# Another order of the block sums in the Winograd product of a hybrid decoder trunk, and shorter filler between its HGRN2 cores' steps

## The chip, the core and the metric

The kernel runs on one core of one Trainium2 chip. Its engines run side by side, each with its own queue: TensorE (PE in the profile, its weight loads PEld), VectorE (DVE), ScalarE (ACT), GpSimd (POOL) and SyncE (SP), which issues the transfers from HBM. The time is the device time of one execution in microseconds; the median of three executions is compared.

## What is computed

A decoder trunk of two layers over 512 tokens with 1024 features. Layer 0 mixes tokens with a Mamba-2 state-space mixer, layer 1 with HGRN2; each layer then has a squared-ReLU MLP and a gate with an embedding of its own. The change touches the border of the two layers and the HGRN2 mixer. Of the reference, cut to this:

```python
for i in range(DEPTH):
    mix = ssd_mixer(x, ...) if i % 2 == 0 else hgrn2_mixer(x, ...)
    h = layer_norm(DEEPNORM_ALPHA * x + mix, ...)
    h = layer_norm(DEEPNORM_ALPHA * h + sq_relu_mlp(h, w1, w2), ...)
    x = h + jax.nn.sigmoid(h @ ple_w_gate[i]) * (p[i] @ ple_w_proj[i])

def hgrn2_mixer(u, w_in, lb, norm_w, w_out):
    q, fz, v, g = jnp.split(u @ w_in, 4, axis=-1)
    k = (1.0 - lb) * jax.nn.sigmoid(-fz)          # and log_f, the decay
    # per head: causal scores of q and k under the decay, times v; state from chunk to chunk
    ...
    o = rms_norm(o, norm_w) * jax.nn.silu(g)
    return o @ w_out
```

## The kernel before

Every float32 product is made of three matmuls on operands that are split into a high and a low part (`mm3`, L118 to L120: high by high, high by low, low by high). ACT writes a high part, DVE subtracts it from the value for the low part. For weights `unit` loads a piece of 128 x 1024 through SP (L105) and `split` makes the parts (L112 on ACT, L114 on DVE).

The instructions of an engine stand in an order that a planner makes beforehand: among those that are ready, the one that comes first in the program goes first, and `tc.high_priority(offset=n)` lets an instruction count as n places earlier. Within `tc.manual_schedule` for PE (around the call of `values4`, L814, and around the cores, L1069) TensorE's own order is that of the program; the other engines' orders are still planned.

**The gate of layer 0** (`mlp_and_gate`, L464 to L502) works through two halves of the features, h, and four token chunks, c. After each chunk's output the chunk before it is transposed (`turn`, L442): four transposes by TensorE (L447), the high part of the transposed tokens (L450, ACT), a float32 copy into `rows` (L451, ACT) and the low part (L452, DVE). `rows[0]` holds tokens 0 to 255, `rows[1]` tokens 256 to 511, each with both halves of the features. The last `turn`, of h = 1 and c = 3, is left over in `late`.

**`values4`** (L505) computes the values and output gates of the first four HGRN2 heads, X W with X of 512 tokens x 1024 features, by seven products of blocks (Winograd's form of Strassen's method) in place of eight. The blocks of X are a11 and a12 (tokens 0 to 255, first and second half of the features) and a21 and a22 (tokens 256 to 511), views of `rows`, 128 x 1024 each in memory. The products in TensorE's order, 24 matmuls each: a11 (then the left-over `turn`), a12, s3, s2, a22, s1, s4, where

- s1 = a21 + a22
- s2 = s1 - a11
- s3 = a11 - a21
- s4 = a12 - s2

`put` (L512) splits a sum into a buffer of the pool `b8` (L514 on ACT, L515 on DVE). The sums of the weights t1 to t4 are made by `weight_sums` (L314) and split in `sums(t)`. `first` (L532, ACT) and `more` (L535, DVE) take results out of PSUM; at the end a Silu is applied to the gates' half (L560, ACT).

**The HGRN2 cores.** `hcore` (L930) handles two heads; it runs four times, for heads 0, 2, 4 and 6. It has 15 steps, after each of which it yields: seven levels m = 0 to 6 (L949 and L963 are the matmuls of levels 0 to 4, L970 of levels 5 and 6; DVE scales with L983 and L984; ACT copies scores with L1006 after level 4 and with L1012 at levels 5 and 6), two steps of transposed keys (L1019, copied by L1021), two of states `sv` (L1030, L1032, L1034), two of outputs `po` (L1043, L1045, squares and square root L1050 and L1051 on ACT, L1055 on DVE) and two of transposed outputs `ot` (L1063, taken out by L1064 on ACT and L1065 on DVE, through the one bank `pt`).

Between the steps TensorE gets filler from `background`: the projections of the next heads, q0 to q7 (`qf`, 16 pieces each), the values of the last four heads, v2 and v3 (`vg`, 32 pieces each), and the first half of the output projection, o (`out0`, 32 pieces). A piece is one `mm3` of three matmuls of 512 columns and counts as 0.65. `fill(n)` adds n to a credit and takes pieces while it is positive. The n of a step is its entry of `FILL`, in the fourth core times LAST = 0.78; before the first core q0 and q1 are made and 6.0 (`AHEAD`) filled. What a job leaves for ACT when its last matmul is done is its tail: four activations for a `qf` (L880, L881, L883, L884), copies and Silus for a `vg` (L861, L863). What the background has left after the fourth core runs then; the second half of the output projection (`out_project`, L82) isn't under the manual order and is planned into TensorE's free places.

Of the kernel before, what the change touches and what calls it, by code (L numbers as in the profile page):

```python
# [27 lines left out]
RAWS = 3  # L28
FIRST = 1000
SOON = 40  # L30

PERIODS = ("TTTTTTTT",) + 3 * ("TTQTQTQTQTQTQTQ",) + ("QQQQQQQ",)
SUMS = (60, 300, 300, 300)

JOBS = "q2 q3 q4 q5 v2 q6 q7 v3 o".split()
FILL = (3.15, 1.1, 1.35, 1.95, 2.4)
VALUE_SUMS = 60
AHEAD = 6.0
LAST = 0.78
# [4 lines left out]
def trunk(ctx: ExitStack, tc, a):  # L44
    nc = tc.nc
# [21 lines left out]
    def mk(p, shape, tag, dt=F32, **kw):  # L67
        return p.tile(list(shape), dt, tag=tag, name=nm(tag), **kw)

    def f32(t):  # L70
        return t.bitcast(F32)
# [19 lines left out]
    def bank(p, tag):  # L91
        return mk(p, [P, T], tag)
# [8 lines left out]
    def unit(src, lead=LEAD):  # L101
        n = src.shape[1]
        with tc.high_priority(offset=lead):
            raw = mk(raws, [P, 1024], "raw")
            nc.sync.dma_start(raw[:, :n], src)  # L105
        return split(raw[:, :n], lead)

    def split(f, lead=LEAD):
        n = f.shape[1]
        with tc.high_priority(offset=lead):  # L110
            hi = mk(whip, [P, 1024], "whi", F32R)
            nc.scalar.copy(hi[:, :n], f)  # L112
            lo = mk(wlop, [P, 1024], "wlo", F32R)
            nc.vector.tensor_sub(lo[:, :n], f, f32(hi[:, :n]))  # L114
        return hi, lo

    def mm3(out, sh, sl, mh, ml, start, stop, **kw):
        nc.tensor.matmul(out, sh, mh, start=start, stop=False, **kw)  # L118
        nc.tensor.matmul(out, sh, ml, start=False, stop=False, **kw)  # L119
        nc.tensor.matmul(out, sl, mh, start=False, stop=stop, **kw)  # L120
# [77 lines left out]
    def layer_norm(c, gb, sums=None):  # L198

        src = acc[:, c, :]  # L200
        mv = mk(sm, [P, 2], "lnmv")
        sd = mk(sm, [P, 1], "lnsd")
        if sums is None:
            st = mk(sm, [P, 2, 6], "lnst")
            for h in range(2):
                nc.vector.bn_stats(st[:, h, :], src[:, h * 512 : (h + 1) * 512])
            nc.vector.bn_aggr(mv, st.rearrange("p a b -> p (a b)"))
            nc.scalar.activation(sd, mv[:, 1:2], AF.Sqrt, bias=eps)
        else:

            nc.vector.tensor_scalar(mv[:, 0:1], sums[:, c, 0:1], sums[:, c, 1:2], -1.0 / D, ALU.add, ALU.mult)
            sq = mk(sm, [P, 2], "lnsq")
            for h in range(2):
                nc.scalar.activation(
                    tmp("sg", [P, T]), src[:, h * 512 : (h + 1) * 512], AF.Square, bias=mv[:, 0:1], accum_out=sq[:, h : h + 1]
                )
            nc.vector.tensor_add(mv[:, 1:2], sq[:, 0:1], sq[:, 1:2])
            nc.scalar.activation(sd, mv[:, 1:2], AF.Sqrt, scale=1.0 / D, bias=eps)
        rs = mk(sm, [P, 1], "lnrs")
        nc.vector.reciprocal(rs, sd)  # L220
        shift = ALU.subtract if sums is None else ALU.add
        nc.vector.scalar_tensor_tensor(src, src, mv[:, 0:1], gb[0], shift, ALU.mult)
        nc.vector.scalar_tensor_tensor(src, src, rs, gb[1], ALU.mult, ALU.add)

    def transpose_split(src, dst, c):

        sl = slice(c * P, (c + 1) * P)
        for q in range(2):
# [5 lines left out]
            h = dst.hi[q][:, :, sl]  # L234
            with tc.high_priority(offset=SOON):
                nc.scalar.copy(h, v)  # L236
# [3 lines left out]
    def out_part(units, n, xs, c, h, first, scale, last=False, sums=None):  # L240
# [8 lines left out]
        d = acc[:, c, h * 512 : (h + 1) * 512]  # L249
        with tc.high_priority(offset=SOON if last else 0):  # L250
            if scale is not None:
# [25 lines left out]
    def norm(i):  # L277
# [5 lines left out]
        def chunk(c):  # L283
            with tc.high_priority(offset=SOON if c < 2 or i % 2 == 0 else 0):
                layer_norm(c, gb, sums)
# [28 lines left out]
    def weight_sums(w, lead, eng=nc.vector):  # L314

        t = [[None, None] for _ in range(4)]

        def load(i, u, src):
            t[i][u] = tmp("r", [P, 1024])
            nc.sync.dma_start(t[i][u], src)  # L320

        with tc.high_priority(offset=lead):
            for u in range(2):
                load(0, u, w[0][1][u])
                load(2, u, w[1][1][u])
                eng.tensor_sub(t[2][u], t[2][u], t[0][u])
                load(1, u, w[0][0][u])
                eng.tensor_sub(t[0][u], t[0][u], t[1][u])
                eng.tensor_add(t[1][u], t[2][u], t[1][u])
            for u in range(2):  # L330
                load(3, u, w[1][0][u])
                eng.tensor_sub(t[3][u], t[3][u], t[1][u])
        return t

    def block_product(w, blk, lead, first, after=None, turns=None, sums=None):
# [7 lines left out]
        def product(x, f, name, start, i, j, turns=None):  # L343
# [4 lines left out]
            for c in range(2):  # L348
# [9 lines left out]
                d = acc[:, 2 - 2 * i + c, j * 512 : (j + 1) * 512]  # L358
                with tc.high_priority(offset=SOON if after else 0):
                    if after and f in (w[1][0], t1, t4, w[1][1]):  # L360
# [144 lines left out]
    def values4(xs, rows, late):  # L505

        w = [[[a["whvg"][4 * j + 2 * i + u] for u in range(2)] for j in range(2)] for i in range(2)]
        t1, t2, t3, t4 = weight_sums(w, VALUE_SUMS, nc.vector)
        a11, a12, a21, a22 = (rows[i][:, j] for i in range(2) for j in range(2))
        res = [[mk(w4, [P, 2, T], "ab"[i]) for i in range(2)] for _ in range(2)]  # L510

        def put(f):  # L512
            t = mk(b8, [P, 2, 4, 256], "b8", F32R)
            nc.scalar.copy(t[:, 0], f)  # L514
            nc.vector.tensor_sub(t[:, 1], f, f32(t[:, 0]))  # L515
            return lambda k, c: tuple(t[:, i, k, c * P : (c + 1) * P] for i in range(2))

        def part(i, j):
            sl = lambda c: slice((2 * i + c) * P, (2 * i + c + 1) * P)
            return lambda k, c: (xs.h(4 * j + k, sl(c)), xs.l(4 * j + k, sl(c)))  # L520

        def product(x, us, banks, start, drain):
            for c in range(2):
                for k in range(4):
                    hi, lo = us[k // 2]
                    ks = slice(k % 2 * T, (k % 2 + 1) * T)
                    mm3(banks[c], *x(k, c), hi[:, ks], lo[:, ks], start and k == 0, k == 3, skip_group_check=True)
                with tc.high_priority(offset=SOON):
                    drain(c, banks[c])

        def first(i, j):
            return lambda c, ps: nc.scalar.copy(res[j][i][:, c], ps)  # L532

        def more(i, j):
            return lambda c, ps: nc.vector.tensor_add(res[j][i][:, c], ps, res[j][i][:, c])  # L535

        pair = lambda: [bank(psj, "pj") for _ in range(2)]
        sums = lambda t: [split(v) for v in t]
        x, z, y = [bank(psy, "py%d" % c) for c in range(2)], pair(), pair()
        product(part(0, 0), [unit(v) for v in w[0][0]], x, True, first(0, 0))  # L540
        for f in late:
            f()
        nc.vector.tensor_add(a22, a21, a22)
        nc.vector.tensor_sub(a21, a11, a21)
        s3 = put(a21)
        product(part(0, 1), [unit(v) for v in w[1][0]], z, True, more(0, 0))
        nc.vector.tensor_sub(a11, a22, a11)
        s2 = put(a11)
        product(s3, sums(t3), y, True, first(1, 1))
        product(s2, sums(t2), x, False, first(1, 0))  # L550
        s1 = put(a22)
        product(part(1, 1), sums(t4), y, False, more(1, 0))
        nc.vector.tensor_sub(a12, a12, a11)
        s4 = put(a12)
        product(s1, sums(t1), x, False, more(1, 1))
        product(s4, [unit(v) for v in w[1][1]], x, False, first(0, 1))
        for j in range(2):
            for i in range(2):
                g = res[j][i][:, :, 256:]
                nc.scalar.activation(g, g, AF.Silu)  # L560
            made["vg", j] = res[j]
# [368 lines left out]
    def hcore(h0, s, i0):  # L930
# [22 lines left out]
        for m in range(NLEV):  # L953
# [35 lines left out]
            for r in R:  # L989
# [17 lines left out]
                else:  # L1007
                    pc = pc[:, base(half) : base(half) + 2 * half].rearrange("p (c l) -> p c l", c=2)
                    for b in range(0, P, 2 * half):
                        for odd in range(2):  # L1010
                            row = b + half * odd
                            nc.scalar.copy(sc[b : b + half, odd::2, b + half : b + 2 * half], pc[row : row + half])  # L1012
            yield FILL[0]

        kt = []
        for r in R:
# [4 lines left out]
            nc.scalar.copy(kt[r], pt[:, : 3 * P].rearrange("p (c k) -> p c k", c=3))  # L1021
            yield FILL[1]
        res = need("vg", h0 // 2)
# [3 lines left out]
        for r in R:  # L1027
# [5 lines left out]
            for c in range(1, 3):  # L1033
                nc.vector.scalar_tensor_tensor(  # L1034
                    sv[r][:, c], sv[r][:, c - 1], tot[r][:, c : c + 1], pss[:, c * P : (c + 1) * P], ALU.mult, ALU.add
                )
            yield FILL[2]
        os = []
        for r in R:
# [18 lines left out]
            os.append(o)  # L1058
            yield FILL[3]
        for r in R:  # L1060
# [4 lines left out]
            nc.vector.scalar_tensor_tensor(s.l(i0 + r), pt, hnw[:, 0:1], f32(s.h(i0 + r)), ALU.mult, ALU.subtract)  # L1065
            yield FILL[4]

# [136 lines left out]
```

## Time and profile before

| | |
|---|---|
| median of 3 executions | 1437.37 us (1437.36 to 1441.27) |
| the profiled execution | 1437.35 us, its span 1435.5 us |
| mean granted clock of TensorE | 0.997 |
| transfers | 176.69 MB on the queue for data, 35.6% of 16 DMA engines' time |
| the gate of layer 0 (its last part) | about 715 to 765 us |
| `values4` | about 765 to 811 us |
| the four cores with their filler | about 840 to 1026 us |

Times within the execution are counted from the span's start. An instruction on a line of a helper, such as L118, belongs to whoever called it, so the tiles' names tell the place: `pj` and `py` are PSUM banks, `whi` and `wlo` the parts of weights, `b` the pool of split tokens, `blk` the rows. [...]

### The profile page before, as it was taken

To read this page: it belongs to the slowest core of one execution; us is meant where nothing else is said; L and a number is where in the kernel's file an instruction comes from. 1 tells how busy PE (TensorE), PEld (TensorE's weight loads), DVE (VectorE), ACT (ScalarE), POOL (GpSimd) and SP (SyncE) were. 2 spreads that over 40 slices of the span, in tenths; PEclk is the share of its full clock that TensorE was granted. 3 is DMA by queue.
4 is the path that set the end of the run, shared out by engine and by line. 5 is a ranking of instruction groups with operands and counts; after the bars stand their busy time and mean duration, and the time that the engine had idled before them with its cause. 6 is when DMAs were issued, how large, how long until landed. Compare 5 with 4: busy or idle time off the path is not lost.

```text
span 1435.5 us, 20976 instructions
## 1 busy us (share of the span) xinstructions
PE 1420.1 (99%) x8381; PEld 1175.9 (82%) x8381; DVE 1039.9 (72%) x1664; ACT 746.0 (52%) x1117; POOL 1.9 (0%) x12
## 2 busy tenths in 40 slices
PE   9999999999999999999999999999999999999998
PEld 7888888888888888888887877778798888888887
DVE  8998686797967667687967455556786867667873
ACT  7776464662364444445546546554555454544551
POOL 0000000000000000000000000000000000000000
PEclk9999999999999999999999999999999999999999
DMA  8432323334234434345521422212063344434231
GB/s 306 146 118 102 119 90 116 103 104 156 109 123 142 147 132 147 132 147 193 173 74 47 140 82 75 75 62 103 30 235 117 136 143 147 136 137 168 89 118 44
DMA packets 49394, 178.04 MB, mean 124 GB/s; under 512 B 5520, under 2 KB 6288, under 8 KB 49168
## 3 DMA queue, kind: packets, MB, share of 16 engines
q1 hardware_dynamic: 49296, 176.69, 35.6%
q8 instruction: 66, 1.08, 0.3%
q14 instruction: 32, 0.26, 0.1%
HBM read 174.51 MB, written 2.16 MB: 123 GB/s over the span
## 4 chain that ended last, share of the span: by engine, by line
PE 93%; DVE 3%; ACT 3%; issue 1%; ACTq 0%; DVEq 0%
PE pj L118 24%; PE pj L119 23%; PE pj L120 23%; PE py L118 5%; PE py L119 5%; PE py L120 5%; PE py L733 1%; PE py L739 1%; PE pt L232 1%; PE pm L703 1%; PE py L963 1%; DVE wlo L114 1%; PE pt L691 1%; PE py L1043 0%; ACT sc L1012 0%
## 5 line engine op out<-in xcount | busy, mean ns | idle before, releaser
L112 ACT CAST whi<-raw 128x1024 fp32r<-128x1024 f32 x222 | 232.9, 1051 | 349.9 <-PE pj L119 235.1
L118 PE MATMUL pj<-b,whi 128*128 128x512 f32 (+1 forms) x1006 | 382.8, 381 | 0.7 <-ACT b L236 0.7
L119 PE MATMUL pj<-b,whi 128*128 128x512 f32 (+1 forms) x1006 | 380.3, 378 | 0.0
L120 PE MATMUL pj<-b,wlo 128*128 128x512 f32 (+1 forms) x1006 | 379.6, 378 | 0.0
L114 DVE TENSOR_TENSOR wlo<-raw,whi 128x1024 fp32r<-128x1024 f32 x222 | 269.7, 1220 | 144.2 <-ACT whi L112 139.2
L120 PEld LDWEIGHTS pj<-b,wlo 128*128 128x128 f32 x1006 | 189.4, 188 | 33.8
L118 PEld LDWEIGHTS pj<-b,whi 128*128 128x128 f32 x1006 | 189.1, 188 | 34.2 <-ACT b L236 1.1
L118 PE MATMUL pj<-whi,b 128*128 128x512 f32 x536 | 214.5, 400 | 2.1 <-ACT b L514 2.1
L119 PEld LDWEIGHTS pj<-b,whi 128*128 128x128 f32 x1006 | 189.6, 188 | 32.5 <-issue 0.9
L120 PE MATMUL pj<-whi,b 128*128 128x512 f32 x544 | 214.1, 394 | 1.4 <-DVE b L515 1.4
L119 PE MATMUL pj<-wlo,b 128*128 128x512 f32 x536 | 211.0, 394 | 0.0
L120 PEld LDWEIGHTS pj<-whi,b 128*128 128x128 f32 x544 | 102.6, 189 | 23.4 <-DVE b L515 2.2
L118 PEld LDWEIGHTS pj<-whi,b 128*128 128x128 f32 x536 | 101.3, 189 | 23.1 <-ACT b L514 2.5
L119 PEld LDWEIGHTS pj<-wlo,b 128*128 128x128 f32 x536 | 101.3, 189 | 19.5
L112 ACT CAST whi<-r 128x1024 fp32r<-128x1024 f32 x72 | 75.9, 1054 | 68.0 <-PE pj L120 38.8
L114 DVE TENSOR_TENSOR wlo<-r,whi 128x1024 fp32r<-128x1024 f32 x72 | 87.7, 1220 | 24.3 <-ACT whi L112 23.8
L120 PE MATMUL py<-whi,b 128*128 128x512 f32 (+1 forms) x250 | 96.9, 388 | 0.0
L119 PE MATMUL py<-wlo,b 128*128 128x512 f32 x224 | 87.2, 389 | 0.0
L118 PE MATMUL py<-whi,b 128*128 128x512 f32 x224 | 87.0, 390 | 0.0
L120 PEld LDWEIGHTS py<-whi,b 128*128 128x128 f32 x250 | 46.9, 188 | 9.7
L632 DVE SCALAR_TENSOR_TENSOR cv<-pj,cst,cv 128x509 f32<-128x509 f32 (+2 forms) x66 | 48.6, 744 | 3.5 <-ACT cv L629 2.8
L118 PEld LDWEIGHTS py<-whi,b 128*128 128x128 f32 x224 | 42.1, 188 | 9.1 <-DVE sg L493 0.3
(284 smaller groups left out, 1827.0 us busy)
## 6 DMA issues: line engine op xcount, KB each, us to landing
raw<-in_w SPq DMA_DIRECT2D x112, 512.0 KB, 3.2
r<-in_w SPq DMA_DIRECT2D x64, 512.0 KB, 3.3
raw<-in_wssd SPq DMA_DIRECT2D x36, 512.0 KB, 3.3
a<-csd SPq DMA_DIRECT2D x16, 512.0 KB, 3.6
raw<-in_wso SPq DMA_DIRECT2D x16, 512.0 KB, 3.2
raw<-in_wg SPq DMA_DIRECT2D x16, 512.0 KB, 3.3
raw<-in_whq SPq DMA_DIRECT2D x16, 512.0 KB, 3.3
raw<-in_whvg SPq DMA_DIRECT2D x14, 512.0 KB, 3.2
```

The source lines that it names most:

```text
L112: nc.scalar.copy(hi[:, :n], f)
L114: nc.vector.tensor_sub(lo[:, :n], f, f32(hi[:, :n]))
L118: nc.tensor.matmul(out, sh, mh, start=start, stop=False, **kw)
L119: nc.tensor.matmul(out, sh, ml, start=False, stop=False, **kw)
L120: nc.tensor.matmul(out, sl, mh, start=False, stop=stop, **kw)
L232: nc.tensor.transpose(pt[:, j * P : (j + 1) * P], src[:, k * P : (k + 1) * P], ident)
L632: nc.vector.scalar_tensor_tensor(cv[:, d:], ps[:, : T - d], convw[:, i, k : k + 1], cv[:, d:], ALU.mult, ALU.add)
L691: nc.tensor.transpose(pt[:, c * P : (c + 1) * P], xs[:, c * P : (c + 1) * P], ident)
L703: nc.tensor.matmul(pst_[:, c * P : (c + 1) * P], btok[:, c, :], xw[:, c].rearrange("p h q -> p (h q)"), start=True, stop=True)
L733: nc.tensor.matmul(yd[64 * r : 64 * r + 64, sl], xdt[:, 2 * c + r, :], m[:, r, sl], start=True, stop=True)
L739: nc.tensor.matmul(yo[:, c * P : (c + 1) * P], pv[:, c - 1].rearrange("p h q -> p (h q)"), cm[:, c * P : (c + 1) * P], start=True, stop=True,)
L963: nc.tensor.matmul(pcs[r][bs, at], kk[r][:, ts], second(qd[r][:, ts], half), start=True, stop=True)
```

## The change

Two things are altered. In `values4` the four sums of blocks are formed in another order and in other places: s3 first, into a11, at a priority of 60 places earlier, ahead of the first product; then, after the second product, s1 = a21 + a22 into a21 and s2 into a22, now as a22 - s3, which is the same as s1 - a11; s4 from a12 and s2 before the product on a22. The products and TensorE's order of them stay. And the five entries of `FILL` become smaller by about 6 to 7.5%.

```diff
+EARLY = 60
...
-FILL = (3.15, 1.1, 1.35, 1.95, 2.4)
+FILL = (2.94, 1.03, 1.27, 1.83, 2.22)
...
         x, z, y = [bank(psy, "py%d" % c) for c in range(2)], pair(), pair()
+        with tc.high_priority(offset=EARLY):
+            nc.vector.tensor_sub(a11, a11, a21)
+            s3 = put(a11)
         product(part(0, 0), [unit(v) for v in w[0][0]], x, True, first(0, 0))
         for f in late:
             f()
-        nc.vector.tensor_add(a22, a21, a22)
-        nc.vector.tensor_sub(a21, a11, a21)
-        s3 = put(a21)
         product(part(0, 1), [unit(v) for v in w[1][0]], z, True, more(0, 0))
-        nc.vector.tensor_sub(a11, a22, a11)
-        s2 = put(a11)
+        nc.vector.tensor_add(a21, a21, a22)
+        nc.vector.tensor_sub(a22, a22, a11)
+        s2 = put(a22)
         product(s3, sums(t3), y, True, first(1, 1))
+        s1 = put(a21)
         product(s2, sums(t2), x, False, first(1, 0))
-        s1 = put(a22)
+        nc.vector.tensor_sub(a12, a12, a22)
+        s4 = put(a12)
         product(part(1, 1), sums(t4), y, False, more(1, 0))
-        nc.vector.tensor_sub(a12, a12, a11)
-        s4 = put(a12)
         product(s1, sums(t1), x, False, more(1, 1))
         product(s4, [unit(v) for v in w[1][1]], x, False, first(0, 1))
```

## The prediction

> **What bounds the kernel now.** I read the page first: the busy shares and the chain that ended last.
>
> ```profile
> span 1435.5 us, 20976 instructions
> PE 1420.1 (99%) x8381; PEld 1175.9 (82%) x8381; DVE 1039.9 (72%) x1664; ACT 746.0 (52%) x1117; POOL 1.9 (0%) x12
> PE 93%; DVE 3%; ACT 3%; issue 1%; ACTq 0%; DVEq 0%
> ```
>
> TensorE is busy nearly throughout and carries 93% of the chain, and the change takes no matmul away. So it can only win where TensorE stands still or runs on a lower clock. The second view is a table of stretches: the gate, values4, and then the four cores of the HGRN stage. Columns: stretch, its length, busy time of PE, PEld, DVE, ACT, POOL with instruction counts, granted clock, DMA share, GB/s.
>
> ```profile
> 715.00:765.00 50.00, 50.00 (x243) 41.41 (x242) 31.84 (x40) 22.10 (x33) 0.00 (x0) 1.00 0.20 65
> 765.00:811.00 46.00, 42.49 (x178) 33.90 (x177) 32.60 (x34) 28.24 (x35) 1.28 (x4) 0.93 0.27 91
> 840.00:891.00 51.00, 50.09 (x602) 40.39 (x593) 29.16 (x81) 27.55 (x67) 0.00 (x0) 1.00 0.22 74
> 891.00:943.00 52.00, 49.11 (x584) 39.57 (x576) 29.09 (x81) 30.18 (x70) 0.00 (x0) 1.00 0.21 72
> 943.00:993.00 50.00, 50.00 (x589) 40.45 (x587) 30.60 (x83) 25.78 (x64) 0.00 (x0) 1.00 0.25 86
> 993.00:1026.00 33.00, 31.97 (x506) 25.02 (x506) 23.17 (x62) 13.84 (x48) 0.00 (x0) 1.00 0.20 66
> ```
>
> The gate has no idle time. values4 idles 46.00 - 42.49 = 3.51 us and is the one stretch with a clock below 1.00. The cores idle 0.91, 2.89, 0 and 1.03 us, 4.83 in all. These two places are what the change touches.
>
> **The values4 stall.** TensorE in order of time (start, length, line, tiles, idle time before it in brackets), then two stretches around it and one for comparison from the second core:
>
> ```profile
> 775.79 0.39 PE L120 MATMUL pj<-whi,b 128*128 128x512 f32 x1
> ...
> 776.47 0.39 PE L120 MATMUL pj<-whi,b 128*128 128x512 f32 x1
> 778.94 0.64 PE L118 MATMUL pj<-whi,b 128*128 128x512 f32 x1 [2.08 <-ACT b L514]
> 779.38 0.63 PE L119 MATMUL pj<-wlo,b 128*128 128x512 f32 x1
> 781.43 0.80 PE L120 MATMUL pj<-whi,b 128*128 128x512 f32 x1 [1.43 <-DVE b L515]
> ...
> 786.15 0.40 PE L119 MATMUL pj<-wlo,b 128*128 128x512 f32 x1
> ```
>
> ```profile
> 775.68:779.10 3.42, 1.34 (x7) 0.80 (x6) 3.39 (x4) 3.10 (x4) 0.00 (x0) 1.00 0.00 0
> 779.10:785.92 6.82, 5.39 (x13) 3.70 (x14) 6.79 (x7) 3.71 (x4) 0.00 (x0) 0.50 0.00 0
> 936.10:939.53 3.43, 2.21 (x10) 1.49 (x8) 1.14 (x2) 3.42 (x6) 0.00 (x0) 1.00 0.37 135
> ```
>
> Three matmuls normally take 776.47 - 775.79 = 0.68 us, so one takes 0.227. The product on s3 starts at 778.94 instead of 776.70, waiting for the two copies that `put` makes of s3 (L514 the high part, L515 the low part). A stretch of 3.42 us in which TensorE was busy for only 1.34 is followed by 6.82 us at half clock, in which 13 matmuls are touched. The matmul at 786.15 is the 14th after 776.47; unhindered it would have started at 776.47 + 14 x 0.227 = 779.65. **The stall costs 786.15 - 779.65 = 6.5 us**: 3.5 of idleness and 3.0 of clock.
>
> What made s3 late is in the chain that ended last, in order of time:
>
> ```profile
> 773.70 0.68 DVE b L452
> 774.38 0.60 DVE a L535
> 774.98 1.14 DVE blk L543
> 776.15 1.22 DVE blk L544
> 777.37 2.27 DVE wlo L114 x2
> 779.64 0.60 DVE a L535
> 780.24 1.14 DVE b L515
> ```
>
> The first sum, L543, needs a22, which the last transposes deliver just before 773.70; L544 (s3 itself, a11 - a21) stands behind it on DVE although it needs nothing of a22.
>
> **Part 1, the other order.** Four sums and four `put`s before, four and four after; no matmul, DMA or byte is added. The first sum is now s3 = a11 - a21, taken 60 instructions early. Its last input is the copy to the token rows of the fourth first-half transpose; DVE and ACT rows of the gate:
>
> ```profile
> 744.05 0.60 ACT L451 COPY blk<-pt 128x512 f32<-128x512 f32 x1
> ```
>
> ```profile
> 750.99 0.69 DVE L493 TENSOR_TENSOR sg<-py,sg 128x512 f32<-128x512 f32 x1 [5.26 <-ACT sg L486]
> ```
>
> From 744.65 on s3 can be made, and DVE has a gap of 5.26 us before 750.99. One sum (1.22, as L544) and the low part (1.14, as L515) fit in it; ACT's high part is 1.04 (L514, below). I cost this move at nothing: the gate's matmuls hide it. Without that cover it would be 3.4 us on the way to s3, which even then starts at the gate's end at about 765 and is done before 776.70. So s3's wait of 6.5 us goes.
>
> What is late next is **s2**, which still needs a22. Its chain is the one above with the same rows: L452, L535, a21 + a22 in L543's place, a22 - s3 in L544's, the two L114, L535, and s2's low part, done at 780.24 + 1.14 = 781.4. The high part depends on ACT:
>
> ```profile
> 777.84 1.04 ACT L514 CAST b<-blk 128x1024 fp32r<-128x1024 f32 x1
> 778.90 1.28 ACT L560 ACT_TABLE_LOAD   x1
> 780.28 0.63 ACT L560 ACTIVATE a<-a 128x512 f32<-128x512 f32 x1
> ```
>
> It is done at 778.9. TensorE wants s2 after s3's 24 matmuls: 776.70 + 24 x 0.227 = 782.14, and the low part two matmuls later, 782.6. The margin is 3.2 and 1.2 us. If the order puts L560's load and one activation (1.28 + 0.63) ahead of the copy, the high part is ready at 780.8 and the low one near 783.1: 0.5 us of waiting. Bounds 0 to +0.5; I take 0, the rows' own order. s1 and s4 are wanted 48 and 72 matmuls after s2 and their sums stand next to it: no closer. **Part 1: -6.5 us.**
>
> **Part 2, shorter filler.** A piece of filler is three matmuls (0.68 us; the code counts 0.65). FILL sums to 35.65 per core before (7 x 3.15 + 2 x (1.1 + 1.35 + 1.95 + 2.4)) and 33.28 after. Of q2..q7, v2, v3 and o there are 192 pieces, of which 11 run ahead of the first core. Following `credit` step by step, the cores get 55, 54, 55 and 17 pieces before and 51, 51, 51 and 28 after: **11 pieces, 7.5 us, move from the first three cores into the fourth**. Before, they run out after the fourth core's level 4; now after its first `sv` step. The pieces take their weight loads on SP and the splits of those (L112, L114) along, later than before and at DMA shares of 0.20 to 0.25, so they are no wait of their own. Total TensorE work is the same, so only waits count:
>
> ```profile
> PE pt L1063 <- DVE b L1065: 2.3, 1, 2.3
> PE pt L1019 <- ACT btok L1021: 1.4, 2, 0.8
> PE py L970 <- ACT sc L1012: 1.2, 3, 0.5
> ...
> DVE cv L983 <- PE py L963: 19.0, 13, 2.7
> ```
>
> These are waits in the HGRN stage (in all, times, longest). At levels 1 to 4 it is DVE that waits for TensorE, 19.0 / 13 = 1.46 us each time, over twice the 0.68 that one piece fewer takes away: free. The steps in which ACT takes part decide, and there it matters where a background job's tail falls on ACT:
>
> ```profile
> 935.50 1.28 ACT L880 ACT_TABLE_LOAD   x1
> ...
> 939.09 0.69 ACT L1064 ACTIVATE b<-pt,cst 128x512 fp32r<-128x512 f32 x1
> ```
>
> ```profile
> 940.61 0.66 PE L1063 MATMUL pt<-cst,cbm 128*128 128x128 f32 x4 [2.30 <-DVE b L1065]
> 1012.50 0.45 PE L970 MATMUL py<-qd,cv 128*64 128x64 f32 x8 [0.26 <-ACT sc L1012]
> 1016.06 0.55 PE L1019 MATMUL pt<-cst,cv 128*128 128x128 f32 x3 [0.78 <-ACT btok L1021]
> ```
>
> In the second core q6's last piece falls in the second `po` step; its tail (a table load and four activations, 935.50 to 939.09) stands ahead of L1064 and costs 2.3 us. With the new numbers q6 ends in the last `ot` step, where no transposes follow: -2.3. The fourth core's two waits, 0.26 + 0.78, have filler now: about -0.8. Against that, q3 still ends in level 4 of the first core, now with one piece fewer in that step: up to +0.68, taken +0.4. v3 now ends in the third core's `po` and `ot` steps, where its table load and one activation (1.28 + 0.63, as L560) can stand before an L1064, a Sqrt load after it: 0 to +3.2, taken +1.2, the middle being 1.6 and the third core idle 0 so far. Sum -2.3 - 0.8 + 0.4 + 1.2 = **-1.5 us**. Bounds: all idleness of the cores gone, -4.8; all 11 pieces uncovered, 7.5, less the fourth core's 1.0, +6.5.
>
> **Sum.** The profiled execution took 1437.35 us (span 1435.5, 1.85 around it), the median is 1437.37, so no correction. 1437.35 - 6.5 - 1.5 = **1429.4 us**.
>
> [...]
>
> **Rivals.**
> - s2 takes s3's place. If something puts 3 us or more into its chain, TensorE idles again at 782 and the clock falls again: up to 6.5 us back, 1435.9. Against it, the margins of 3.2 and 1.2 us.
> - The early sum isn't early, because `put` finds no free buffer or DVE's order keeps it behind L543: part 1 gives nothing, 1437.35 - 1.5 = 1435.9. Against it, the 20 us between 744.65 and 765.
> - Thin filler. The pieces taken from the first three cores leave waits: 1429.4 plus up to 8.0 (from -1.5 to +6.5), 1437.4 at worst, 1433 in the middle. For it, the ACT tails above; against it, the 1.46 us of DVE's waits.
> - **Slower.** A job's tail stands before a core's ACT step as at 939.09, but TensorE, with a piece fewer in the window, falls from 2.21 us of work to under about 1.34 of 3.4 and the clock halves. Price of one event: 2.3 idle + (6.82 - 1.43) / 2 = 2.7 of clock, 5.0 us. One in each of the first three cores, less the 2.3 already there: +12.7, 1437.35 - 6.5 + 12.7 = 1443.6. It decides from the third such event; for it, a wait of this kind exists today; against it, the clock is 1.00 in all four cores.
>
> **Chances.** A measurement here tells about 0.3% (4.3 us) from no change: faster is under 1433.1, slower over 1441.7. Forecast 0.70, own range 1426.1 (-6.5 - 4.8) to 1432.9; s2 late 0.07; not early 0.04; thin filler 0.12, half of it still faster; slower 0.07. So faster 0.76, same 0.17, slower 0.07. The range goes from 1426 to 1436, taking in both cases at 1435.9 and leaving out the worst of the filler and the slower case.
>
> **What would show it.** Right: s3's sum and `put` lie before 765; no wait for L514/L515's successors at the third product; clock 1.00 through values4; the transposes of the second core's last step without their 2.3 us wait; filler until the fourth core's `sv`. Wrong: any stretch at half clock after 715, an idle gap near the second `ot` step of the third core, or a wait at the product on s2.

## The result, and the profile after

The median is 1428.53 us (1427.82 to 1429.55, 4 executions) against 1438.73 us (1437.36 to 1441.27, 4 executions) for the kernel before: a ratio of 0.9928, 95% interval 0.991 to 0.9945. So the change made the kernel faster by 0.7%, about 10 us. The profiled execution took 1427.82 us, forecast 1429.4; before it was 1437.35. Its span, the busy shares and the chain that ended last, from the page of the changed kernel:

```profile
span 1426.0 us, 20980 instructions
...
PE 1416.5 (99%) x8381; PEld 1174.3 (82%) x8381; DVE 1040.9 (73%) x1664; ACT 746.1 (52%) x1118; POOL 1.9 (0%) x12
...
PE 94%; DVE 3%; ACT 2%; DMA 0%; issue 0%; SPq 0%; ACTq 0%; DVEq 0%
```

The work is the same, 8381 instructions of TensorE; the span is 9.5 us shorter. To see where, compare stretches that begin and end at the same instructions. The tables below do that, first the kernel before, then the changed one: a stretch from the last transpose of the gate to the first core's first matmul, then from each core's first matmul to the next core's, then about the fourth core. Columns as in the prediction: stretch, length, busy time and count of PE, PEld, DVE, ACT, POOL, granted clock, DMA share, GB/s.

```profile
771.11:839.78 68.67, 65.16 (x277) 52.61 (x275) 41.03 (x54) 38.40 (x48) 1.28 (x4) 0.95 0.28 96
839.78:890.83 51.05, 50.14 (x588) 40.44 (x587) 29.14 (x82) 27.38 (x67) 0.00 (x0) 1.00 0.22 74
890.83:943.27 52.44, 49.55 (x585) 39.74 (x584) 29.27 (x81) 30.47 (x71) 0.00 (x0) 1.00 0.21 71
943.27:993.04 49.77, 49.77 (x588) 40.45 (x587) 30.60 (x83) 25.70 (x64) 0.00 (x0) 1.00 0.25 86
993.04:1026.00 32.96, 31.93 (x506) 25.02 (x506) 23.17 (x62) 13.80 (x48) 0.00 (x0) 1.00 0.20 66
```

```profile
771.31:833.43 62.12, 62.12 (x277) 51.17 (x275) 38.54 (x52) 37.03 (x47) 1.28 (x4) 1.00 0.31 106
833.43:881.51 48.08, 47.37 (x577) 38.28 (x576) 28.89 (x81) 26.01 (x65) 0.00 (x0) 1.00 0.22 75
881.51:929.38 47.87, 47.28 (x576) 38.12 (x575) 28.37 (x80) 27.96 (x66) 0.00 (x0) 1.00 0.20 66
929.38:977.43 48.05, 47.45 (x576) 38.04 (x575) 29.85 (x81) 28.88 (x69) 0.00 (x0) 1.00 0.27 94
977.43:1017.00 39.57, 39.33 (x541) 31.26 (x541) 26.87 (x68) 16.02 (x49) 0.00 (x0) 1.00 0.20 68
```

Three things are to be read here. **The stretch with values4** (the first row) holds the same 277 instructions of TensorE in 62.12 us instead of 68.67: -6.55 us, with no idle time and clock 1.00. **The first three cores** hold 11, 9 and 12 instructions of TensorE fewer, 32 in all, as 11 pieces of three matmuls do: that work went behind, into the fourth core. **Idle time** in the cores (length less PE's busy time) is 0.71, 0.59, 0.60 and 0.24 us, 2.14 in all, after 0.91, 2.89, 0 and 1.03, 4.83 in all. The stretch with values4 began 0.20 us later in the execution and the span ended 9.51 us earlier (1435.55 and 1426.04 in the traces), so the part behind it gained 9.51 + 0.20 - 6.55 = 3.16 us.

What feeds the products on s3 and s2, DVE and then ACT in order of time, with two later stretches of ACT in the cores, and then TensorE where the product on s2 begins, with two places in the cores. Lines are numbered one or two higher than before: L542 is s3's sum, L548 and L549 those of s1 and s2, L515 and L516 the copies of `put`, L562 the Silu, L1065 the transposed outputs, L1066 their copy on ACT, L882 and L865 the tails of q6 and v3.

```profile
745.84 1.22 DVE L542 TENSOR_TENSOR blk<-blk,blk 128x1024 f32<-128x1024 f32 x1
...
753.12 1.22 DVE L516 TENSOR_TENSOR b<-blk,b 128x1024 fp32r<-128x1024 f32 x1
...
776.35 1.22 DVE L549 TENSOR_TENSOR blk<-blk,blk 128x1024 f32<-128x1024 f32 x1
...
780.36 2.35 DVE L516 TENSOR_TENSOR b<-blk,b 128x1024 fp32r<-128x1024 f32 x2
```

```profile
751.99 1.08 ACT L515 CAST b<-blk 128x1024 fp32r<-128x1024 f32 x1
...
778.06 2.00 ACT L515 CAST b<-blk 128x1024 fp32r<-128x1024 f32 x2
...
780.55 1.28 ACT L562 ACT_TABLE_LOAD   x1
...
927.42 0.69 ACT L1066 ACTIVATE b<-pt,cst 128x512 fp32r<-128x512 f32 x1 [2.39 <-PE pt L1065]
...
929.64 1.28 ACT L882 ACT_TABLE_LOAD   x1
...
971.43 1.28 ACT L865 ACT_TABLE_LOAD   x1
...
973.26 0.67 ACT L1066 ACTIVATE b<-pt,cst 128x512 fp32r<-128x512 f32 x1
```

```profile
782.34 0.39 PE L119 MATMUL py<-whi,b 128*128 128x512 f32 x1
...
926.79 0.60 PE L1065 MATMUL pt<-cst,cbm 128*128 128x128 f32 x4
...
974.77 0.66 PE L1065 MATMUL pt<-cst,cbm 128*128 128x128 f32 x4 [0.60 <-DVE b L1067]
```

s3's sum and both copies are done by 753.12 + 1.22 = 754.34, inside the gate; the low part comes one gap of DVE later than the sum. s2's sum ends at 777.57, its high part at about 779 (one of the two copies of 778.06) and its low part at about 781.5, half of the row at 780.36; the product on s2 starts at 782.34 without a wait. In the second core's last transposes (926.79) the bracket with 2.30 us of before is gone, because q6's tail (929.64) now comes behind that step's L1066 (927.42). In the third core v3's table load (971.43), and its first activation behind it, stand ahead of an L1066, and the transposes of 974.77 wait 0.60.

### The profile page after: what moved, and what is told of

The parts are those of the page before. It is cut to its first block, busy times and chain, and to the rows that moved or that the text cites. A ratio compares the mean times of both kernels' runs of the same rounds, so it can differ in the third digit from the quotient of the medians.

```text
span 1426.0 us, 20980 instructions
## 1 busy us (share of the span) xinstructions
PE 1416.5 (99%) x8381; PEld 1174.3 (82%) x8381; DVE 1040.9 (73%) x1664; ACT 746.1 (52%) x1118; POOL 1.9 (0%) x12
## 4 chain that ended last, share of the span: by engine, by line
PE 94%; DVE 3%; ACT 2%; DMA 0%; issue 0%; SPq 0%; ACTq 0%; DVEq 0%
PE pj L119 24%; PE pj L120 23%; PE pj L121 23%; PE py L119 5%; PE py L121 5%; PE py L120 5%; PE py L735 1%; PE py L741 1%; PE pm L705 1%; PE py L965 1%; PE pt L233 1%; DVE wlo L115 1%; PE pt L693 1%; PE py L1045 0%; DMA r<-in_w 0%
## 5 line engine op out<-in xcount | busy, mean ns | idle before, releaser
L115 DVE TENSOR_TENSOR wlo<-raw,whi 128x1024 fp32r<-128x1024 f32 x222 | 269.9, 1220 | 142.2 <-ACT whi L113 136.8
L115 DVE TENSOR_TENSOR wlo<-r,whi 128x1024 fp32r<-128x1024 f32 x72 | 87.7, 1220 | 24.1 <-ACT whi L113 23.6
```

## The experiments

Each kernel was run beside the kernel before on the same chip; ratios are to that, with 95% intervals.

**Each part alone.** First the new order with the old filler:

```diff
-FILL = (2.94, 1.03, 1.27, 1.83, 2.22)
+FILL = (3.15, 1.1, 1.35, 1.95, 2.4)
```

> The new order of the block sums with the old FILL. Theory: the two parts are independent, and this one is worth the stall at the product on s3 and its half clock, 6.5 us: span near 1435.5 - 6.5 = 1429.0, clock 1.00 throughout values4, the waits of the four cores as before the change (2.3 us at the second core's last transposes, 4.8 us of idleness in all). Rival: the filler's position depends on what happens in values4, so that the waits of the cores change with the order alone; then the span is not 1429.0 and the 2.3 us wait is gone or another one has come.

Median 1431.19 us, ratio 0.9958 (0.9946 to 0.9971). Then the old order with the new filler, the same two lines the other way round in the kernel before:

> The old order with the new FILL. Theory: span 1435.5 - 3.0 = 1432.5, the rest of the 9.5 us by which the changed kernel's span is shorter; the stall at the product on s3 stays with 6.8 us of half clock. Rival 1: shorter filler gains nothing by itself (1435.5), the 9.5 us come from the order. Rival 2: it costs, up to 6.5 us (1442).

Median 1435.23 us, ratio 0.9977 (0.9968 to 0.9986). Against their 1438.33 the parts are worth 7.1 and 3.1 us; the sum, 10.2, is what both give together (1438.73 - 1428.53 = 10.2). So in the medians the parts add up, and the filler is worth twice what was forecast.

In the profile of the first, the stretch with values4 gained the same 6.55 us, but the wait at the second core's last transposes, which the old filler leaves there, did more harm than in the kernel before. TensorE there, then the stretch around the wait and the one behind it:

```profile
934.87 1.11 PE L1065 MATMUL pt<-cst,cbm 128*128 128x128 f32 x4 [2.29 <-DVE b L1067]
```

```profile
931.38:934.80 3.42, 1.20 (x6) 0.65 (x4) 0.86 (x2) 2.65 (x5) 0.00 (x0) 1.00 0.46 153
934.80:938.21 3.41, 3.34 (x10) 2.86 (x11) 0.76 (x2) 0.69 (x1) 0.00 (x0) 0.50 0.00 0
```

2.29 us of idleness, 2.30 before: the same wait. Here it left only 1.20 us of work in a stretch of 3.42 and was followed by 3.41 us at half clock; before, the stretch quoted in the prediction held 2.21 and the clock stayed. Of the five executions, three had a mean clock of 1.000 and spans of 1429.0 to 1429.4, two 0.998 and 1431.4 and 1432.0. The profiled one is the 1431.4; where the other of the two lost its clock no trace shows. What such a wait costs thus depends on when it falls.

**Does s3 have to be early, or only first?** The sum and its `put` go behind the left-over transposes in the program, without a raised priority:

```diff
-        with tc.high_priority(offset=EARLY):
-            nc.vector.tensor_sub(a11, a11, a21)
-            s3 = put(a11)
...
         for f in late:
             f()
+        nc.vector.tensor_sub(a11, a11, a21)
+        s3 = put(a11)
```

> The changed kernel without EARLY: s3's sum and put stand behind the left-over transposes, at no priority, s3 still formed first and without a22. Theory: the dependence on a22 was what made s3 late, not its place in the program; the sum runs in the same gap of the gate as soon as its inputs are there, and the span is that of the changed kernel, 1426.0 within 0.5. Rival: the early place is what counts; s3 then waits behind the last transposes and the stall returns in part, 1428 to 1433.

Median 1428.43 us, ratio 0.9932 (0.9919 to 0.9946): the changed kernel's time. DVE in its gate (L544 is s3's sum here):

```profile
746.07 1.22 DVE L544 TENSOR_TENSOR blk<-blk,blk 128x1024 f32<-128x1024 f32 x1
```

The sum stands in the same gap of the gate as in the changed kernel. The place in the program and the priority do nothing: the planner takes what is ready, and s3 is ready once it doesn't have to follow a sum that needs a22.

The opposite, the old order (s3 behind the sum of a22) with the new filler and that block raised by 200 places, so that it is late but goes ahead of everything else:

```diff
-        nc.vector.tensor_add(a22, a21, a22)
-        nc.vector.tensor_sub(a21, a11, a21)
-        s3 = put(a21)
+        with tc.high_priority(offset=200):
+            nc.vector.tensor_add(a22, a21, a22)
+            nc.vector.tensor_sub(a21, a11, a21)
+            s3 = put(a21)
```

> The old order and sums with the new FILL, but the two sums and the put that lead to s3 at a priority of 200 places, ahead of the split of t4 on DVE. s3 then comes about 2.4 us earlier than before and TensorE idles about 1.0 and 0.6 us instead of 2.08 and 1.43. Theory A: what trips the clock is how little TensorE was busy in a stretch of 3.4 us, and with about 1.8 us of idleness (1.6 busy or more) it stays at 1.00: loss 2 us, span near 1426.0 + 2 = 1428. Theory B: any stall here halves the clock: 1426.0 + 2 + 2.5 to 3 = 1431. Without the earlier place it would be near 1432.5.

Median 1437.17 us, ratio 0.9992 (0.9984 to 1.0001): 1.9 us slower than the new filler alone, and slower than both theories expected. The wait at s3's high part shrank from 2.1 us (new filler alone) to 0.8, but one of 2.6 came at the product on s2, as the list of TensorE's waits of this kernel shows (in all, times, longest); below it DVE's sum for s2 (L548), and ACT up to the copy that s2's product needs:

```profile
PE py L118 <- ACT b L514: 2.6, 1, 2.6
...
PE pj L118 <- ACT b L514: 0.8, 1, 0.8
```

```profile
781.64 1.21 DVE L548 TENSOR_TENSOR blk<-blk,blk 128x1024 f32<-128x1024 f32 x1
```

```profile
785.66 1.05 ACT L112 CAST whi<-r 128x1024 fp32r<-128x1024 f32 x1 [0.87 <-PE pj L120]
787.03 1.05 ACT L112 CAST whi<-r 128x1024 fp32r<-128x1024 f32 x1 [0.32 <-PE pj L120]
...
788.46 2.94 ACT L514 CAST b<-blk 128x1024 fp32r<-128x1024 f32 x3
```

s2's sum was ready at 782.85, its copy started at 788.46: ahead of that copy stood two copies of weights (L112), which themselves waited for TensorE (the brackets), and two copies of results out of PSUM (784.21 and 787.99, not shown). Two stretches at half clock came out of it, one behind each group of waits:

```profile
777.24:780.65 3.41, 1.59 (x7) 0.82 (x6) 3.41 (x4) 3.19 (x3) 0.00 (x0) 1.00 0.00 0
780.65:784.06 3.41, 3.41 (x10) 2.63 (x9) 3.38 (x4) 0.63 (x1) 0.00 (x0) 0.50 0.00 0
787.48:790.89 3.41, 0.80 (x3) 0.37 (x3) 3.06 (x4) 3.41 (x5) 0.00 (x0) 1.00 0.00 0
790.89:794.30 3.41, 3.41 (x8) 2.73 (x9) 2.15 (x2) 0.51 (x1) 1.14 (x4) 0.50 0.00 0
```

**How far is s2 from taking s3's place?** The changed kernel with two sums more in s2's chain (a11 added to it and taken away again):

```diff
         nc.vector.tensor_add(a21, a21, a22)
+        nc.vector.tensor_add(a22, a22, a11)
+        nc.vector.tensor_sub(a22, a22, a11)
         nc.vector.tensor_sub(a22, a22, a11)
         s2 = put(a22)
```

> The changed kernel with two more DVE operations in s2's chain (s3 is added to a22 once and taken off again): 2 x 1.2 us later, so the low part of s2 is ready near 784.0 instead of 781.6, and wanted at 782.8. Theory (the margin of s2 is 1.2 us): TensorE waits about 1.2 us at the second matmul group of the product on s2, too little to halve the clock; span 1427.2. Rival 1 (s2 isn't close to the path): no wait, 1426.0. Rival 2 (any wait there halves the clock): 1430 or more.

Median 1435.4 us, ratio 0.9977 (0.9968 to 0.9986), 6.9 us above the changed kernel, where the theory expected 1.2 and the second rival 4 or more. DVE from the two added sums (L549, L550) over the sum of s2 (L551) to the low part (L516); then the stretch at the product on s2 and the next:

```profile
777.71 1.22 DVE L549 TENSOR_TENSOR blk<-blk,blk 128x1024 f32<-128x1024 f32 x1
778.86 1.22 DVE L115 TENSOR_TENSOR wlo<-r,whi 128x1024 fp32r<-128x1024 f32 x1
...
780.59 1.21 DVE L115 TENSOR_TENSOR wlo<-r,whi 128x1024 fp32r<-128x1024 f32 x1
781.73 1.22 DVE L550 TENSOR_TENSOR blk<-blk,blk 128x1024 f32<-128x1024 f32 x1
782.98 1.23 DVE L551 TENSOR_TENSOR blk<-blk,blk 128x1024 f32<-128x1024 f32 x1
784.12 2.35 DVE L115 TENSOR_TENSOR wlo<-r,whi 128x1024 fp32r<-128x1024 f32 x2
...
787.53 3.49 DVE L516 TENSOR_TENSOR b<-blk,b 128x1024 fp32r<-128x1024 f32 x3
```

```profile
783.95:787.36 3.41, 0.73 (x2) 0.30 (x2) 3.41 (x4) 3.40 (x4) 0.00 (x0) 1.00 0.00 0
787.36:794.19 6.83, 5.39 (x13) 4.23 (x14) 3.66 (x4) 1.66 (x3) 1.28 (x4) 0.50 0.00 0
```

The two added sums are 2.44 us of work, yet s2's sum, which ended at 777.57 in the changed kernel, ends at 784.21 here, 6.64 later: between the first added sum and the second, and again ahead of the low part of s2, the planner put low parts of weights (L115). TensorE idled 3.41 - 0.73 + 6.83 - 5.39 = 4.12 us and, by an estimate that takes half of the busy time at clock 0.50 as lost, (6.83 - 1.44) / 2 = 2.7 more to the clock, 6.8 together, about the 6.9 by which the medians differ. The rival "s2 takes s3's place" is thus real, and its price is about that of the old stall; in the changed kernel it doesn't happen.

**What the half clock cost.** The kernel before, with idle time at s3 filled by matmuls whose result nobody reads: 10 ahead of the product's first matmul and 8 ahead of its third (`idle(n)` issues them).

```diff
+                        idle(warm[0])
...
+                        idle(warm[1])
...
-        product(s3, sums(t3), y, True, first(1, 1))
+        product(s3, sums(t3), y, True, first(1, 1), (10, 8))
```

> The kernel before, with the stall at the product on s3 filled by matmuls whose results nobody reads: 10 of 512 columns before the product (10 x 0.227 = 2.3 us) and 8 between its second and third matmul (1.8 us). They take nothing away from what s3 waits for. Theory: of the 6.5 us, 3.5 are idleness and 3.0 the halved clock, so that the same wait at full clock costs 3.5: span 1435.5 - 3.0 = 1432.5, clock 1.00 in values4. Rival: the half clock follows from something other than an idle TensorE and stays, or the 3.0 us were data that would have been late anyway; span 1435.5 or more.

Median 1436.65 us, ratio 0.9981 (0.9972 to 0.999). From the last transpose of the gate to the first core:

```profile
772.52:839.05 66.53, 66.53 (x295) 54.41 (x293) 40.97 (x54) 38.22 (x48) 1.28 (x4) 1.00 0.29 99
```

With the clock kept at 1.00 the stretch takes 66.53 us instead of 68.67, and 62.12 without the wait. So the clock's share of the 6.55 us is 2.14, where 3.0 was expected, and the wait itself is worth 66.53 - 62.12 = 4.41. That figure would be the filling's own length if the matmuls put in had outlasted the wait. They didn't: the product's first matmul (L532 in this kernel) and its third (L535) start as their operands are done, the low part at 781.56 + 1.22 = 782.78 and the high part, by an estimate, near 780.29 (777.84 + 1.04 = 778.88 in the kernel before, and 772.52 - 771.11 = 1.41 later here):

```profile
780.37 0.49 PE L532 MATMUL pj<-whi,b 128*128 128x512 f32 x1
...
782.83 0.50 PE L535 MATMUL pj<-whi,b 128*128 128x512 f32 x1
```

**Where the filler's gain comes from.** Two theories: the filler was too thick, or it only matters in which step a job's tail falls. The changed kernel with the old thick filler, started 4.0 later, so that the tails fall elsewhere:

```diff
-FILL = (2.94, 1.03, 1.27, 1.83, 2.22)
+FILL = (3.15, 1.1, 1.35, 1.95, 2.4)
...
-AHEAD = 6.0
+AHEAD = 2.0
```

> The new order with the old, long FILL, but AHEAD = 2.0 in place of 6.0: the first three cores keep 54, 55 and 55 pieces, and every job ends some 6 pieces later, q6 in the second core's last `ot` step as in the changed kernel. Theory (where a job's tail falls decides): the 2.3 us wait at the second core's last transposes goes, though the filler is as thick as before; span 1426 to 1428, clock 1.00. Rival (the amount decides): with the long filler the wait stays and the span is that of the new order alone, 1429.0, or 1431 to 1432 with a halved clock.

Median 1431.06 us, ratio 0.9948 (0.9935 to 0.996). The waits of its cores, from 830 to 980 us:

```profile
PE pt L1065 <- DVE cbm L1057: 1.5, 1, 1.5
PE pt L1065 <- DVE b L1067: 1.0, 1, 1.0
```

The 2.3 us wait is gone though the filler is as thick as before; waits of 1.5 and 1.0 stand at other transposes, the first in the first core and the second in the third. Of its five executions two had a mean clock of 1.000 and spans of 1427.5 and 1428.5, three 0.999 and 1429.3 to 1431.3. Only the profiled one, 1427.5, has a trace, so where the others lost their clock stays open. The theory expected 1426 to 1428: the profiled execution is in it, the median isn't.

The other way: the changed kernel, its thin filler started 5.0 earlier, so that q6's tail falls ahead of the second core's last transposes again:

```diff
-AHEAD = 6.0
+AHEAD = 11.0
```

> The changed kernel with AHEAD = 11.0: FILL stays short (52, 51 and 51 pieces in the first three cores), but q6 ends in the second core's second `po` step again, as before the change. Theory (tail): a wait of 2 to 3 us at that core's last transposes comes back, and with it a halved clock in some runs; span 1428 to 1432, 2 to 5 above the changed kernel's 1426.0. Rival (amount): no such wait, 1426 to 1427.

Median 1435.18 us, ratio 0.9976 (0.9966 to 0.9985): 6.7 us above the changed kernel, more than the 2 to 5 expected. The transposes, and the two stretches there:

```profile
937.21 0.66 PE L1065 MATMUL pt<-cst,cbm 128*128 128x128 f32 x4 [4.12 <-DVE b L1067]
```

```profile
934.47:937.89 3.42, 0.68 (x5) 0.69 (x6) 0.83 (x2) 3.41 (x5) 0.00 (x0) 1.00 0.00 0
937.89:941.30 3.41, 3.41 (x9) 2.68 (x9) 1.89 (x2) 0.81 (x3) 0.00 (x0) 0.50 0.33 114
```

The wait came back where it was put, larger than the 2.3 us of before, and took the clock with it: 4.12 + 3.41 / 2 = 5.8 us of the 6.7, by the same estimate. It is the tail's place that decides. ACT's rows also show why the wait is larger here: the tail is mixed with the square root of the `po` step (L1053), and ACT loads three tables (at 929.67, 931.58 and 933.90, 1.28 us each) ahead of the L1066 at 935.68, on which the transposes of 937.21 depend; in the kernel before q6's tail loads one, at 935.50.

Last, still thinner filler, with start and last core set so that no tail falls ahead of a step in which ACT takes part:

```diff
-FILL = (2.94, 1.03, 1.27, 1.83, 2.22)
+FILL = (2.74, 0.957, 1.175, 1.697, 2.088)
...
-AHEAD = 6.0
-LAST = 0.78
+AHEAD = 10.0
+LAST = 0.86
```

> The new order with FILL at 0.87 of the old, AHEAD = 10.0 and LAST = 0.86: 48, 47 and 48 pieces in the first three cores and 32 in the fourth, and the jobs' tails in levels 0 to 3 or last steps, but for q4 and v2 (second step of transposed keys). Theory (tail): another 3 or 4 pieces fewer per core open no wait at levels 1 to 4, where DVE waited 1.46 us each time; the third core's 0.6 us wait goes; span 1424.5 to 1426. Rival (thin filler): the 10 pieces taken out are waits of 0.68 us each; span 1428 to 1433.

Median 1428.52 us, ratio 0.9928 (0.9914 to 0.9941). The first three cores hold 567, 565 and 568 instructions of TensorE, about three pieces each fewer than the changed kernel's 576, and idle 0.37, 0.06 and 0 us; the first of them:

```profile
839.31:884.92 45.61, 45.24 (x567) 36.43 (x566) 27.64 (x80) 25.87 (x66) 0.00 (x0) 1.00 0.21 71
```

So thinner filler leaves no waits by itself. To see whether this version beats the changed kernel, both ran once more side by side:

> The changed kernel once more, beside the next one and the kernel before on the same chip. Theory: 1428.5 in the median, spans of its runs within 1426.0 to 1428, clock 0.999 to 1.00 in each.

> The new order with FILL at 0.87 of the old, AHEAD = 10.0 and LAST = 0.86 once more, to see whether it beats the changed kernel. Its listed waits of TensorE in the cores sum to 1.5 us against 3.0 in the changed kernel. Theory: 1 to 1.5 us faster than the changed kernel in the medians. Rival: no difference beyond the scatter of the runs, because other small changes of order take it back.

The changed kernel: 1429.04 us, ratio 0.9928 (0.9915 to 0.994). The thin one: 1428.29 us, ratio 0.9925 (0.9913 to 0.9938). The intervals cover each other: no difference that these runs can tell, so the expected gain of 1 to 1.5 us isn't there and the rival holds.

## Why the prediction was right, point by point

- **Part 1, -6.5 us: right in size, wrong in its split.** The stretch with values4 gained 6.55. The prediction took the whole from one delay, that of the matmul at 786.15, so the size didn't hang on the split. It divided the whole into 3.5 us of idleness and 3.0 of clock; with the clock kept the split is 4.4 and 2.1. The rows quoted in the prediction hold the reason. s3's low part was done at 780.24 + 1.14 = 781.38, while the third matmul, which needs it, was due at 776.70 + 2 x 0.227 = 777.15: a delay of 4.2 us whatever the clock. The two matmuls ahead of it ran slowly inside that delay (0.44 us from 778.94 to 779.38, in place of 0.227), for nothing. The estimate counted their slowness as a cost of the clock.
- **s3 early in the gate: the place was right, the reason only in part.** The sum lies at 745.84 and its copies before 765, with TensorE still busy for 50.00 of the 50 us from 715 to 765. But "taken 60 instructions early" isn't what does it. Without the priority the sum stands in the same gap and the time is the same. What counts is that s3 no longer follows the sum of a22. The rival "the early sum isn't early" fell with it.
- **s2's margin, taken as no wait: right, but its bound was too small.** The product on s2 starts without a wait, and the table load (780.55) stands behind both copies on ACT (778.06). The bound of +0.5 also doesn't come out of its own rows: with the high part ready at 780.8, the low part would be done at 780.8 + 1.14 = 781.9 and not "near 783.1", ahead of the 782.6 at which it is wanted. And it treated lateness as if it grew by as much as the chain grows. The run with 2.44 us more in the chain lost 6.9: s2's sum fell behind other work in the planned order of DVE, and then the clock fell. The price that the rival "s2 takes s3's place" was given, up to 6.5 us, was the better figure.
- **Part 2, -1.5 us: right in sign, and half of what was measured, -3.16.** By the idle time of the cores the first gave -0.20 (taken +0.4), the second -2.30 (taken -2.3), the third +0.60 (taken +1.2), the fourth -0.79 (taken -0.8); these add up to -2.69. Two terms were mis-sized: the first core lost nothing with one piece fewer in its level 4, and v3's tail in the third core cost half of what was taken. Behind the cores TensorE idled 0.35 us more than before (409.04 - 404.60 = 4.44 after 409.55 - 405.46 = 4.09), so idle time gives -2.34 in all. The other 0.82 is busy time, 586.03 us instead of 586.85 for the same 4174 instructions; why stays open.
- **11 pieces move: right.** 32 instructions of TensorE fewer in the first three cores; 11 pieces are 33.
- **Where the tail falls: shown.** Thick filler without the tail there has no such wait, thin filler with the tail there has one of 4.12 us. The rival "thin filler leaves waits" fell with the still thinner version.
- **The slower rival: its mechanism exists, and the change took it away.** A job's tail ahead of an ACT step can take the clock down, as in the run with the old filler (1.20 us busy in a stretch of 3.42, then clock 0.50) and in the one with the tail put back (0.68 us). The prediction asked for three such events in the changed kernel; it has none, and its clock is 1.00 in every row shown.
- **A sign of being wrong that did show.** The prediction named an idle gap near the second `ot` step of the third core as such a sign. There is one, of 0.60 us (974.77), for the reason that its own sum had priced at +1.2: v3's table load ahead of an L1066. So the sign spoke against a term of the prediction itself, and doesn't make it wrong.

## What to carry to other kernels

Look at what a sum depends on before its place in the program: an operand that is ready early is only early if its instruction isn't chained, through a buffer or a shared partial sum, to one that is late. When background work is spread between the steps of a chain, look first at where a job's last instructions fall on the second engine: here thin filler with the tail in the wrong place waited 4.12 us, and thick filler with the tail elsewhere lost the 2.3 us wait. And price a wait of some 2 us on TensorE at up to 1.7 times that, an estimate from the run with the old filler (2.29 of idleness and 3.34 / 2 of clock): there it halved the clock, while one of 2.30 in the kernel before did not.

## What the runs showed of the hardware

In these traces the clock changes on a beat of 3.41 us. In the run with the late s3, for one, it changes at 780.65, 784.06, 790.89 and 794.30, which is one, three and four beats after the first. A stretch of that beat in which TensorE was busy for 0.68, 0.73, 0.80, 1.20, 1.28, 1.34 or 1.59 us was followed by one or two stretches at half clock (3.41 or 6.83 us); one with 2.21 us was not. In the run of the thick filler started later, this one was not either:

```profile
874.98:878.39 3.41, 1.89 (x9) 1.12 (x7) 2.06 (x7) 3.38 (x5) 0.00 (x0) 1.00 0.00 0
```

That it lies on the beat no row shows, since no change of clock near it marks its place. So in these traces the border lies between 1.59 and 2.21 us of work in a stretch, or between 1.59 and 1.89 if it does: 3.41 - 1.59 = 1.8 us of idleness was enough in one run. The same wait of 2.3 us kept the clock in the kernel before, where two stretches shared it (2.21 us busy from 936.10, 2.33 from 939.53), and halved it with the old filler behind the new order, where one stretch held most of it (1.20 us busy). It did so too in the profile of the kernel whose stall was filled (1.28 us busy from 937.75 to 941.16, then 3.41 us at half clock), although its cores are those of the kernel before.

A matmul of 512 columns is recorded as 0.39 us long at clock 1.00, while the next one starts after about 0.23 (782.34, 782.56 and 782.79 in the changed kernel).
